# One hybrid RG-LRU and mLSTM layer: the whole body in a scheduled block of the more detailed timing model

## The chip, the core and the metric

The kernel runs on one core of a Trainium2 chip. The metric is the time of one execution on the device in microseconds, the median of the runs shown. The engines are named as the profile names them: PE (TensorE) for matmuls, DVE (VectorE), ACT (ScalarE), POOL (GpSimd), SP (SyncE). Each takes its own instructions in a fixed order and waits on semaphores for the others. In this kernel SP issues the loads and POOL the stores.

## The reference

One layer (DEPTH 1) with a 1024-token prompt and eight single decode tokens, all float32. `D_MODEL` is 1024, there are four mLSTM heads of 256, and the RG-LRU has 1024 channels in 16 gate blocks of 64.

```python
hn = rmsnorm(x, g_norm)
u = hn @ w_in                                   # 1024 x (7*1024 + 8)
xa, za, uq, uk, uv, uo, zb, ui, uf = jnp.split(u, SPLIT_IDX, axis=-1)
yA, hA, bufA = rglru_branch(xa, conv0, h0, ...) # conv of 4 taps, two gates, linear scan over time
hB, C, n, m = mlstm_seq(q, k, v, ig, lf, C0, n0, m0)   # chunks of 128 tokens, state C 256 x 256 per head
yB = jax.nn.sigmoid(uo) * hB
yB = yB * lax.rsqrt(jnp.mean(yB * yB, axis=-1, keepdims=True) + EPS) * g_mhead
merged = jnp.concatenate([yA * silu(za), yB * silu(zb)], axis=-1)
x = x + merged @ w_out
y = rmsnorm(x, g_final)
```

This is done once for the prompt, from zero states, and once for the eight decode tokens, each from its own stored states. For decode token b and head h the new state is C' = scale * C + outer(weighted k, v); it is an output, and q is multiplied by it.

## The kernel before

**Matmuls.** Every float32 operand is split into a rounded high half and a rest: `split` (L70 a copy on ACT, L71 a subtraction on DVE), and `mm3` (L64 high by high, L65 and L66 high by low and low by high) adds three matmuls into one PSUM tile. PSUM has three tiles of tag `o`, two of `kv`, and one each of `tr`, `s` and `qp`; an instruction that writes one of these waits until its last reader is through.

**The input projection** runs over 14 `UNITS` ("v0v1 x0y0 q0k0 x1y1 ..."), two pieces of 256 columns each. A unit is multiplied in a 2 x 2 block scheme with seven products (`Q_P1` to `Q_P7`) instead of eight. `load_raw` (L223, SP) brings its weights in pieces of 512 KB into raw0 and raw1; `prep` makes the seven combined weight blocks (DVE L261, L262, L264, L270) and splits each into `wh` and `wl`, two products ahead of the one that PE runs (`LEAD`, with `NWS` 6 buffers); `evac` (L307 to L332) takes sums out of PSUM and `emit_out` (L343 to L360) stores them from POOL to scratch in DRAM. `dec_unit` multiplies the decode tokens by the same raw weights: sixteen narrow matmuls L236 into the one `tr` tile, a copy L239 on ACT, four transposes L244.

**Background work** is written between the halves of the products, taken from queues of small steps by `pop_bg`. `rg_half` is the RG-LRU of 128 channels and 512 tokens: convolution (L761 to L767), gate matmuls L784 into the `s` and then the `tr` tile, gate outputs L734 on ACT, decay and scan (L797 to L816). `rg_dec` is its decode part (PE L836, four small L734). L659 belongs to the gate preparation of the mLSTM.

**Decode states.** `decode_steps(h)` goes through the eight tokens of a head. `fetch_C` (L909, SP) brings a state of 256 KB into one of four buffers of tile `Cb`, `fetch_v` (L903, SP) broadcasts v into one of two `vbc`. A token is scaled on ACT (L930), gets two additions on DVE (L932) and is stored from POOL (L934). After every second token a run of eight narrow matmuls (L951) multiplies the two states by q into `ps_qp`.

```python
def token(b):
    ...
        A.mul(C, C, dGI[:, b, h:h + 1])                        # L930
        for kb in range(2):
            V.scalar_tensor_tensor(C[:, kb, :], vb_, ...)      # L932
        stq(s_C[0, b, h].rearrange(...), C)                    # L934
        if b % 2:
            late.append(lambda: late.append(products))         # L951
        else:
            fetch_C(i + 2); fetch_C(i + 3)                     # L909
```

**The last stages.** The mLSTM goes over eight chunks and four heads: `m_a` (L1124 to L1134), `m_b` (matmuls L64 to L66 into `ps_qp`, scaled by L1180 into `hh`), normalisation, `m_z` (L1230). In the first of its chunks `wo_prep` still prepares w_out: loads `oraw` of 512 KB (L1246), the decode tokens' product L1260 into `ps_tr`, the split L1269 on ACT and L1270 on DVE. `out_part` multiplies by w_out.

**What sets the order.** The body only states the operations in a program order. The framework underneath schedules them: among the instructions that could run, it takes them by program order against a timing model, and writes one queue for each engine with the semaphore waits that the tiles need. The engine and queue of every instruction are set by the code; no order is written out by hand beyond the program order.

Of the kernel before, what the change touches and what calls it, by code (L numbers as in the profile page):

```python
# [49 lines left out]
def hymba_kernel(  # L50
# [3 lines left out]
    w_rgate, b_rgate, w_igate, b_igate, lru_lambda, b_mi, b_mf, g_mhead, w_out, g_final,  # L54
    y_p, y_s, p_h, p_conv, p_C, p_n, p_m, s_h, s_conv, s_C, s_n, s_m,
):
    nc = tc.nc
    V, A, G, TE = nc.vector, nc.scalar, nc.gpsimd, nc.tensor
    ld = nc.sync.dma_start
    stq = nc.gpsimd.dma_start  # L60
# [1513 lines left out]
```

## Time and profile before

| what | value |
|---|---|
| median of 3 runs | 953.24 us (953.04 to 954.88) |
| span of the profiled execution | 952.8 us |
| DMA | 153.19 MB, mean 161 GB/s |
| matmul L64 into ps_kv, 128x512 | 320, mean 400 ns each |
| split of a weight block, L70 and L71 | 91 each, mean 1049 and 1220 ns |
| scaling of a decode state, L930 | 32, median 723 ns |

A row of the timeline has start and length in us, engine, line, operation and tiles; in brackets stands the idle time of the engine before it and what ended it. Matmuls overlap, so that two follow each other by less than their length. In the rows of waits stand the engine with the tile and line that waited, what it waited for, the total in us, how often, and the longest. The times of a group of instructions are minimum, median and maximum in ns.

### The profile page before, as it was taken

How to read it: one execution, taken by the hardware profiler on the slowest of the kernel's cores; microseconds unless marked ns; L12 is line 12 of the kernel's file. 1: busy time of each engine (PE TensorE's matmuls, PEld its weight loads, DVE VectorE, ACT ScalarE, POOL GpSimd, SP SyncE). 2: the span in 40 equal slices, each digit the busy share in tenths (PEclk: the TensorE clock that was granted, in tenths of full speed). 3: DMA queues.
4: the chain of work that ended last, by engine and by line, in shares of the span. 5: the costliest groups of instructions: out<-in, count | busy, mean ns of one | idle time of the engine just before them, and what ended most of it. 6: DMA issues, size and time to landing. Idle time of an engine off the chain costs nothing.

```text
span 952.8 us, 15351 instructions
## 1 busy us (share of the span) xinstructions
PE 929.8 (98%) x5350; PEld 762.8 (80%) x5350; DVE 711.5 (75%) x1465; ACT 585.0 (61%) x1050; POOL 145.7 (15%) x259
## 2 busy tenths in 40 slices
PE   9999999999999999999999999999989999999997
PEld 7797767777787987777789998866667888888886
DVE  6685798889788877979797867686656676676764
ACT  7563447778677757677687774465446466455532
POOL 1111112111112122111122221010200100000020
PEclk9999999999999999999999999999999999999999
DMA  5521347356645465455647362435963664564361
GB/s 172 183 82 46 132 123 273 110 182 206 238 146 202 156 206 173 164 159 184 213 146 255 119 219 84 153 111 168 302 193 107 185 179 113 154 184 137 120 102 48
DMA packets 131383, 153.19 MB, mean 161 GB/s; under 512 B 15816, under 2 KB 110056, under 8 KB 131298
## 3 DMA queue, kind: packets, MB, share of 16 engines
q1 hardware_dynamic: 113578, 96.34, 34.5%
q0 software_dynamic: 17728, 55.87, 16.3%
q8 instruction: 42, 0.69, 0.3%
q14 instruction: 35, 0.29, 0.1%
HBM read 100.59 MB, written 51.65 MB: 160 GB/s over the span
## 4 chain that ended last, share of the span: by engine, by line
PE 76%; DVE 9%; DMA 7%; issue 4%; ACT 2%; SPq 1%; POOL 0%; DVEq 0%; POOLq 0%; ACTq 0%
PE ps_o L66 12%; PE ps_o L64 12%; PE ps_o L65 12%; PE ps_kv L64 9%; PE ps_kv L66 9%; PE ps_kv L65 9%; PE ps_tr L236 2%; DMA W<-d_alpha 2%; DMA x<-in_x_prompt_dram 2%; PE ps_s L1124 1%; PE ps_qp L951 1%; DVE wl L71 1%; PE ps_tr L1260 1%; PE ps_s L784 1%; PE ps_qp L64 1%
## 5 line engine op out<-in xcount | busy, mean ns | idle before, releaser
L71 DVE TENSOR_TENSOR wl<-raw,wh 128x1024 fp32r<-128x1024 f32 x91 | 111.0, 1220 | 27.6 <-ACT wh L70 19.0
L70 ACT CAST wh<-raw 128x1024 fp32r<-128x1024 f32 x91 | 95.4, 1049 | 58.1 <-PE ps_o L65 23.6
L64 PE MATMUL ps_kv<-cb_hi,wh 128*128 128x512 f32 x320 | 128.1, 400 | 0.6 <-ACT s L317 0.6
L66 PE MATMUL ps_kv<-cb_hi,wl 128*128 128x512 f32 x320 | 125.6, 393 | 0.0
L65 PE MATMUL ps_kv<-cb_lo,wh 128*128 128x512 f32 x320 | 125.2, 391 | 0.0
L64 PE MATMUL ps_o<-cb_hi,wh 128*128 128x512 f32 x240 | 95.0, 396 | 0.0
L66 PE MATMUL ps_o<-cb_hi,wl 128*128 128x512 f32 x240 | 94.1, 392 | 0.0
L65 PE MATMUL ps_o<-cb_lo,wh 128*128 128x512 f32 x240 | 93.5, 389 | 0.0
L64 PEld LDWEIGHTS ps_kv<-cb_hi,wh 128*128 128x128 f32 x320 | 60.1, 188 | 23.7 <-issue 4.6
L66 PEld LDWEIGHTS ps_kv<-cb_hi,wl 128*128 128x128 f32 x320 | 60.1, 188 | 15.6 <-issue 2.5
L65 PEld LDWEIGHTS ps_kv<-cb_lo,wh 128*128 128x128 f32 x320 | 60.2, 188 | 12.5 <-issue 0.8
L64 PE MATMUL ps_kv<-wh,cb_hi 128*128 128x256 f32 x192 | 55.4, 288 | 0.0
L65 PE MATMUL ps_kv<-wl,cb_hi 128*128 128x256 f32 x192 | 54.3, 283 | 0.0
L66 PE MATMUL ps_kv<-wh,cb_lo 128*128 128x256 f32 x192 | 54.3, 283 | 0.0
L64 PE MATMUL ps_o<-wo,rh 128*128 128x512 f32 (+1 forms) x136 | 53.8, 396 | 0.0
L64 PEld LDWEIGHTS ps_o<-cb_hi,wh 128*128 128x128 f32 x240 | 45.1, 188 | 10.6 <-issue 1.7
L66 PEld LDWEIGHTS ps_o<-cb_hi,wl 128*128 128x128 f32 x240 | 45.0, 188 | 10.6 <-issue 0.8
L66 PE MATMUL ps_o<-wo,ml 128*128 128x512 f32 (+1 forms) x136 | 52.1, 383 | 1.1 <-DVE ml L71 1.0
L64 PE MATMUL ps_o<-wo,mh 128*128 128x512 f32 (+1 forms) x136 | 52.8, 389 | 0.0
L65 PEld LDWEIGHTS ps_o<-cb_lo,wh 128*128 128x128 f32 x240 | 45.1, 188 | 9.2
L66 PE MATMUL ps_o<-wo,rl 128*128 128x512 f32 (+1 forms) x136 | 52.0, 382 | 0.0
L65 PE MATMUL ps_o<-wo,rh 128*128 128x512 f32 (+1 forms) x136 | 51.8, 381 | 0.0
(482 smaller groups left out, 2538.7 us busy)
## 6 DMA issues: line engine op xcount, KB each, us to landing
raw<-in_w_in_dram SPq DMA_DIRECT2D x55, 512.0 KB
Cb<-in_state_mlstm_C_dram SPq DMA_DIRECT2D x32, 256.0 KB
out_dram<-Cb POOLq DMA_DIRECT2D x32, 256.0 KB, 4.7
qk<-d_qk SPq DMA_DIRECT2D x32, 256.0 KB
oraw<-in_w_out_dram SPq DMA_DIRECT2D x16, 512.0 KB
d_qk<-s POOLq DMA_DIRECT2D x24, 256.0 KB, 3.9
d_x<-s POOLq DMA_DIRECT2D x16, 256.0 KB, 2.5
zsr<-d_y SPq DMA_DIRECT2D x16, 256.0 KB
```

The lines of the kernel that those rows point to most:

```text
L64: TE.matmul(out, ah, bh, start=first, stop=False, skip_group_check=True)
L65: TE.matmul(out, ah, bl, start=False, stop=False, skip_group_check=True)
L66: TE.matmul(out, al, bh, start=False, stop=last, skip_group_check=True)
L70: A.copy(hi, src)
L71: V.tensor_tensor(lo, src, hi.bitcast(F32), op=ALU.subtract)
L236: TE.matmul(pz[32 * g:32 * g + 32, :], hnd[:, NB * k:NB * k + 32], raws[u, k // 4][:, k % 4, :], start=k < 4, stop=k >= 4, skip_group_chec ...
L784: TE.matmul(pg, w[:, n, :], st["xx"][n], start=k == 0, stop=k == 1)
L951: TE.matmul(pq[32 * g:32 * g + n, 0:256], q, ds_["C", h * NB + bb][:, kb, :], start=b == 1, stop=b == NB - 1, skip_group_check=True)
L1124: TE.matmul(S, qk[:, 2 + kb, :], qk[:, kb, :], start=kb == 0, stop=kb == 1)
L1260: TE.matmul(dec_o[0][32 * g:32 * g + 32, :], md, oraw[m][:, half * 512:(half + 1) * 512], start=n == 0, stop=n == 14, skip_group_check=True)
```

## The change

The kernel's body is put into one block of the framework, entered at its first line, with a flag by which the order of instructions in that block is chosen against another, more detailed timing model of the engines. No operation, tile, size, engine or queue is changed, and the block covers everything from there to the end of the kernel.

```diff
--- before
+++ after
@@ -54,7 +54,7 @@
-    nc = tc.nc
+    nc = (ctx.enter_context(tc.block(schedule_with_timeline_sim=True)), tc.nc)[1]
     V, A, G, TE = nc.vector, nc.scalar, nc.gpsimd, nc.tensor
     ld = nc.sync.dma_start
     stq = nc.gpsimd.dma_start
```

## The prediction

> **What bounds the kernel now.** I read the page first: busy times, then the chain.
>
> ```profile
> span 952.8 us, 15351 instructions
> PE 929.8 (98%) x5350; PEld 762.8 (80%) x5350; DVE 711.5 (75%) x1465; ACT 585.0 (61%) x1050; POOL 145.7 (15%) x259
> ...
> PE 76%; DVE 9%; DMA 7%; issue 4%; ACT 2%; SPq 1%; POOL 0%; DVEq 0%; POOLq 0%; ACTq 0%
> ```
>
> PE sets the end: 929.8 of 952.8 us are busy, and 23 us are all that a better order could remove. How it runs by stage (stretch, its length, busy us of PE, weight loads, DVE, ACT and POOL, granted clock, DMA share, GB/s), and what it waits for:
>
> ```profile
> 100.00:200.00 100.00, 96.26 (x458) 74.30 (x457) 87.34 (x169) 62.40 (x95) 16.30 (x31) 1.00 0.51 168
> 200.00:300.00 100.00, 100.00 (x483) 77.46 (x482) 88.50 (x150) 74.25 (x105) 21.23 (x37) 1.00 0.61 201
> 400.00:500.00 100.00, 100.00 (x543) 80.30 (x542) 84.98 (x140) 71.52 (x102) 17.17 (x30) 1.00 0.52 168
> 600.00:700.00 100.00, 95.88 (x450) 67.70 (x449) 66.88 (x127) 54.81 (x84) 11.02 (x21) 0.98 0.56 182
> ```
>
> ```profile
> PE ps_qp L64 <- ACT hh L1180: 4.0, 1, 4.0
> PE ps_s L784 <- DVE xh L778: 1.7, 2, 1.3
> PE ps_s L659 <- DVE stk L651: 1.7, 1, 1.7
> ```
>
> From 200 to 300 and from 400 to 500 us PE never stops, with DVE at 85 to 88%: there a new order has nothing to win and much to lose. The three named waits come to 4.0 + 1.3 + 1.7 = 7.0 us. The first also costs clock:
>
> ```profile
> 688.00:696.00 8.00, 3.98 (x28) 2.48 (x27) 3.98 (x8) 3.15 (x7) 0.00 (x0) 1.00 0.98 307
> 696.00:700.00 4.00, 4.00 (x20) 3.71 (x19) 3.73 (x9) 1.91 (x6) 0.00 (x0) 0.57 0.58 147
> 140.00:150.00 10.00, 8.68 (x39) 6.82 (x38) 7.68 (x14) 7.32 (x11) 1.45 (x2) 1.00 1.02 300
> ```
>
> After the stall before 696 PE gets a clock of 0.57 for 4 us, so 0.43 x 4 = 1.7 us more are lost; after the shorter stall inside 140:150 it stays at 1.00. The long one costs 4.0 + 1.7 = 5.7 us.
>
> **What the change moves.** Both kernels hold the same instructions; their compiled order, which is known before a run, differs in 1182 of PE's 5035 places, 636 of DVE's 1465, some 316 of ACT's 938, 101 of SP's 385 loads and 59 of POOL's. No instruction gets cheaper. Each engine takes its queue in order, so a price is what an instruction put in front has to wait for. Four moves matter.
>
> **Move 1: the decode of the first heads is bunched.** A head has eight tokens: a 256 KB state is fetched into one of four Cb buffers (L909), scaled on ACT (L930), added to twice on DVE (L932), stored from POOL (L934) and multiplied on PE (L951, a run of eight for two tokens). The buffer is fetched again when store and product are through.
>
> ```profile
> L951 PE MATMUL ps_qp<-Cb,qsel x24: 379/379/380, 216.6 to 253.8; 128*4 128x256 f32 x24
> L932 DVE SCALAR_TENSOR_TENSOR Cb<-vbc,kw,Cb x12: 456/478/486, 210.9 to 244.1; 128x256 f32<-128x256 f32 x12
> L951 PE MATMUL ps_qp<-Cb,qfirst x8: 379/391/403, 197.3 to 197.6; 128*32 128x256 f32 x8
> L930 ACT ACTIVATE Cb<-Cb,dGI x8: 707/724/728, 202.6 to 259.6; 128x512 f32<-128x512 f32 x8
> DMA to landing us min/median/max: 3.1/4.4/4.8
> DMA to landing us min/median/max: 3.1/4.7/7.4
> ```
>
> (The landings: all decode transfers of 195:260, then the stores L934 of 130:270.) Before, head 0's four products are spread from 197.3 to 253.8 us, and its scalings and the next head's first four reach to 259.6. In the new order all four stand within some 80 places of PE, the first ahead of the L784 that PE runs at 164.2 us, the last before 182; eight scalings stand on ACT ahead of a weight copy that had none of them in front of it:
>
> ```profile
> 165.03 1.28 ACT L734 ACT_TABLE_LOAD   x1
> 168.34 0.68 ACT L734 ACTIVATE rg<-ps_tr,hb 64x512 f32<-64x512 f32 x1
> 169.76 0.82 ACT L797 ACTIVATE na<-rg,sp 128x512 f32<-128x512 f32 x1
> 171.78 0.59 ACT L239 COPY Z<-ps_tr 128x512 f32<-128x512 f32 x1 [0.19 <-PE ps_tr L236]
> 174.28 1.05 ACT L70 CAST wh<-raw 128x1024 fp32r<-128x1024 f32 x1 [0.59 <-DVE raw L262]
> 181.10 1.09 ACT L734 ACTIVATE dgr<-ps_s,hb 64x8 f32<-64x8 f32 x4
> ```
>
> ```profile
> 175.42 1.22 DVE L71 TENSOR_TENSOR wl<-raw,wh 128x1024 fp32r<-128x1024 f32 x1
> 164.22 0.39 PE L784 MATMUL ps_s<-xh,ghi 128*128 128x512 f32 x1
> 182.06 0.39 PE L64 MATMUL ps_o<-cb_hi,wh 128*128 128x512 f32 x1
> ```
>
> The row of 164.22 marks where the bunch begins. The copy of 174.28 (with its low half, DVE from 175.42 to 176.6) feeds the PE product of 182.06: PE has 182.1 - 176.6 = 5.5 us to spare. I follow the new order by hand, starting when PE reaches the first product. A step costs its row; a fetch 3.6 us (between the shortest 3.1 and the median 4.4, which also holds stores), a store 0.7 of issue and 4.7. (1) 164.5 product, fetch of the third pair lands 168.3, scaling to 169.0. (2) table load 1.28, the square root 0.6, second scaling 0.72: 171.6. (3) its two DVE additions, 0.96 by the row's duration: 172.6. (4) store, 0.7 + 4.7: 178.0. (5) the fetch that reuses the buffer, for the next head: 181.6. (6) scaling 0.72, four dgr outputs 1.09, a copy 0.3, two L734 of 0.68: 185.1. On these two waits L236's run on PE, since there is one ps_tr buffer; its place is at PE time 182.1 + about 1.1 already lost, so PE is now 3.0 late. (7) scaling 0.72, two activations of 0.82, the run of L236 beside them, L239 0.59, two L307 of 0.59, the eighth scaling 0.72: 190 at the latest step. (8) the copy 1.05: 191. Its reader's place is now 184.3 (182.1 plus the products moved in front): 6.7 late. (9) Its low half comes behind five small DVE steps and ends at 193.3, for a place at 185.2: 8.1 late. (10) The next piece has L264 and the square root with its table ahead of it and ends some 2 us later than its reader: about 10 late in all. PE does not win this back, since 200:300 leaves it no idle time. Bounds: with the shortest fetch throughout and the DVE steps beside the waits, 6; with 4.4 for each of three fetches and the late copies of the next pieces, 13. I take **+10**, nearest to the chain as it stands.
>
> The same happens to head 2 and the first half of head 3, at 375 to 410 us: the products stand up to 362 places earlier. There the copies are further ahead of PE; the same walk leaves 0 to 3 us of stall, and the load for a later unit, behind four vbc loads on SP, another 0 to 2. I take **+1.5**, bounds 0 and +5.
>
> **Move 2: two early stalls go.** L659 stands 28 places later and the first L784 43 later, at one place per 0.23 us (the step from row to row below) 6 and 10 us of other products. That removes 1.7 + 1.3 and some 0.15 of restart at each: **-3.3**; at worst -1.5, if half of the wait appears again at the new place.
>
> ```profile
> 250.54 0.39 PE L66 MATMUL ps_o<-cb_hi,wl 128*128 128x512 f32 x1
> 250.77 0.39 PE L64 MATMUL ps_kv<-cb_hi,wh 128*128 128x512 f32 x1
> ```
>
>
> **Move 3: the stall at 691.**
>
> ```profile
> 695.64 0.39 PE L64 MATMUL ps_qp<-vh,ph 128*128 128x258 f32 x1 [4.02 <-ACT hh L1180]
> 693.25 1.15 ACT L1269 ACTIVATE wo<-oraw,gm 128x1024 fp32r<-128x1024 f32 x1 [4.85 <-DMA oraw<-in_w_out_dram]
> 695.12 0.47 ACT L1180 ACTIVATE hh<-ps_qp,gi_t 128x257 f32<-128x257 f32 x1
> ```
>
> PE waits for hh, which stands on ACT behind an L1269 that waits 4.85 us for its load. In the new order L1180 stands ahead of the L1269s and the PE group 108 places earlier. So this wait goes, at best 5.7 us. But the load is no faster: 688:696 shows the DMA engines 0.98 busy, and the L1260 products that need these loads stand only 32 to 40 places later, 7 to 9 us. I take **-3.5**, between 0 (PE meets the load at L1260) and -5.7.
>
> **Move 4: more split runs of narrow matmuls.** The order cuts L236 into 17 runs instead of 15, L1260 into 15 instead of 13, L951 into 19 instead of 16.
>
> ```profile
> 216.57 0.62 PE L951 MATMUL ps_qp<-Cb,qsel 128*4 128x256 f32 x8
> 301.60 1.92 PE L236 MATMUL ps_tr<-raw,hnd 128*32 128x512 f32 x16
> 303.46 0.39 PE L64 MATMUL ps_kv<-wh,cb_hi 128*128 128x256 f32 x1
> 26.48 1.90 PE L236 MATMUL ps_tr<-raw,hnd 128*32 128x512 f32 x10 [0.53 <-DVE hnd L425]
> 28.32 0.66 PE L417 MATMUL ps_s<-idF,x 128*128 128x128 f32 x4
> 29.34 1.06 PE L236 MATMUL ps_tr<-raw,hnd 128*32 128x512 f32 x6
> 30.33 0.39 PE L64 MATMUL ps_o<-wph,b12h 128*128 128x264 f32 x1
> ```
>
> Sixteen L236 in one run take 303.46 - 301.60 = 1.86 us; cut into 10 and 6 they take 1.84 + 0.99, so one cut costs up to 0.97. I price an L1260 cut alike, and an L951 cut at 0.4, two thirds of its whole run of 0.62. 2 x 0.97 + 2 x 0.97 + 3 x 0.4 = 5.1 at most, and half of that if a cut falls between equal halves; I take **+4**, bounds 2.5 and 5.1.
>
> **The rest.** At the start the transposes of x stand 44 to 48 places earlier, and in the last stage the first products of each output block 31 to 41; both wait for loads or DVE results as before: **0**, bounds -3 and +3. The new order also alternates more often between the accumulations of two PSUM tiles. I cost that at nothing: from ps_o to ps_kv, 250.54 to 250.77, PE keeps its step.
>
> **The sum**, against the profiled 952.8: +10 + 1.5 - 3.3 - 3.5 + 4 + 0 = +8.7, so 961.5; the median of the runs, 953.24, lies 0.4 above the profiled span: **962**. All low ends: 6 + 0 - 3.3 - 5.7 + 2.5 - 3 = -3.5, 949 to 950. All high ends: 13 + 5 - 1.5 + 0 + 5.1 + 3 = +24.6, 978.
>
> The Trainium skill ("TensorE: Matmul & The Clock Gate", Part 1: The HAM clock gate) says that one idle window of about 3.4 us puts the array to half rate, and that it takes about 3.4 us of work to return. The rows above agree: a stall of 4.0 us cost clock, one of 1.3 did not. By that rule the 6.7 us of lateness in move 1 would cost 1.7 us more if they fell in one piece; as I walk them they fall as 3.0, 3.7, 1.4 and 2, so one half-rate stretch at most, and the sum would be 964.
>
> **The rivals.** (a) *Faster, 947.* The decode is covered after all: if fetches land in 3.1 us and the state copies run in ACT's idle 37% of 100:200, then the 5.5 us to spare are just used up, move 1 costs 2 at most, and 691 gives its full 5.7: 952.8 + 2 + 0 - 3.3 - 5.7 + 2.5 = 948.3, and 947 with 1.5 at the start. For it: ACT is only 62% busy there. Against: the waits are in a row on one queue, and four buffers allow no overlap between pairs. It decides if the copy before 182.06 in the new order starts less than 5.5 us late. (b) *Much slower, 978.* Both bunches cost 10 to 13 us, because the fetches also hold SP's queue ahead of weight loads, and the half clock comes once: 952.8 + 13 + 10 - 3.3 - 0 + 4 + 1.7 = 978. For it: both bunches have the same form and DVE is 85% busy at 400:500. Against: there the copies have more lead. (c) *No change.* The stalls only change places: a gain of 7 at the named waits against 7 in the bunch. It needs terms that cancel to 2 us.
>
> **How the numbers follow.** The forecast (cost of the bunch outweighs the stalls removed) 0.58, (b) 0.13, (c) 0.07, (a) 0.22. Slower by over 0.2% (1.9 us, about what can be told from no change) 0.58 + 0.13 - 0.01 = 0.70, the 0.01 being the tail of the forecast that ends under it; faster 0.22 + 0.01 = 0.23, same 0.07. The forecast's own range is 955 to 974; to hold 8 in 10, it reaches into both rivals: 946 to 979.
>
> **What would show it.** PE waits between 165 and 205 us for ACT's L930 or the copy L70 behind it, some 10 us in all; in 200:300 PE at 100% again; no wait for hh L1180 of 4 us and PEclk at 1.00 around 690; no wait at L659 and L784 near 126 and 143; PE busy time up by about 4 us. I am wrong if PE has no wait over 1 us between 165 and 205, if the hh wait is still there, or if the L909 fetches do not come bunched.

## The result and the profile after

The changed kernel takes 998.7 us, the median of four runs (995.17 to 1004.23), against 953.14 us of the kernel before on the same chip: a ratio of 1.0484, interval 1.0461 to 1.0507. It is slower by 4.8%, some 46 us, and lies above the predicted range of 946 to 979. The profiled execution is the slowest of the four (1004.23 us, mean clock 0.978); the other three had 0.982 to 0.987, so the share of the clock below is on the high side. The span and the busy times of its page:

```profile
span 1002.5 us, 15384 instructions
PE 954.0 (95%) x5350; PEld 775.1 (77%) x5350; DVE 714.2 (71%) x1465; ACT 581.6 (58%) x1050; POOL 146.0 (15%) x259
```

DVE and ACT do the same work as before, to within 4 us (711.5 and 585.0). PE is busy 954.0 instead of 929.8 us with the same 5350 instructions, and idle for 48.5 instead of 23.0. So the 50 us of span come half from waiting (25.5) and half from matmuls that took longer (24.2). Most of the second half is the clock: its mean went from 0.994 to 0.978, which is 0.006 x 952.8 = 5.7 us lost before and 0.022 x 1002.5 = 22.1 now. Where it happens, by stretches of 100 us (columns as before: length, busy us of PE, weight loads, DVE, ACT, POOL, granted clock, DMA share, GB/s):

```profile
100.00:200.00 100.00, 90.77 (x414) 65.77 (x413) 73.88 (x135) 52.07 (x84) 18.40 (x33) 0.94 0.52 171
200.00:300.00 100.00, 94.09 (x418) 73.13 (x417) 80.23 (x134) 64.40 (x89) 15.88 (x28) 0.96 0.44 150
300.00:400.00 100.00, 100.00 (x645) 84.23 (x643) 83.62 (x134) 68.61 (x98) 20.81 (x33) 1.00 0.54 176
700.00:800.00 100.00, 94.22 (x470) 70.32 (x467) 60.21 (x142) 49.70 (x110) 10.30 (x19) 0.97 0.61 192
800.00:900.00 100.00, 92.61 (x502) 79.22 (x502) 60.44 (x189) 50.96 (x135) 6.53 (x12) 0.97 0.50 145
```

The last two stretches in the kernel before:

```profile
700.00:800.00 100.00, 99.64 (x550) 82.28 (x549) 65.36 (x199) 54.38 (x145) 7.61 (x14) 1.00 0.51 151
800.00:900.00 100.00, 98.50 (x560) 84.67 (x560) 67.58 (x206) 55.01 (x148) 6.53 (x12) 1.00 0.52 149
```

The losses are local. 300:400 is full; 100:300 and 700:900 lose 28.3 us to waiting (9.23 + 5.91 + 5.78 + 7.39; 5.6 in the kernel before) and 16 to the clock (0.06, 0.04, 0.03 and 0.03 of 100 us; none to two digits before). What PE waits for, in the view of waits:

```profile
PE ps_s L784 <- DVE xh L778: 8.5, 3, 5.9
PE ps_qp L1230 <- ACT hh L1180: 8.0, 3, 4.4
PE ps_tr L236 <- ACT ig L734: 3.6, 1, 3.6
```

**160 to 200 us, the decode bunch.** ACT and PE in the timeline, the rows with a wait, and the windows around them:

```profile
183.75 1.35 ACT L930 ACTIVATE Cb<-Cb,dGI 128x512 f32<-128x512 f32 x2 [5.50 <-DMA Cb<-in_state_mlstm_C_dram]
...
173.80 0.47 PE L784 MATMUL ps_s<-xh,ghi 128*128 128x512 f32 x1 [2.26 <-DVE xh L778]
188.09 3.51 PE L236 MATMUL ps_tr<-raw,hnd 128*32 128x512 f32 x16 [3.62 <-ACT ig L734]
194.86 0.79 PE L64 MATMUL ps_o<-cb_hi,wh 128*128 128x512 f32 x1 [1.88 <-ACT wh L70]
```

```profile
165.00:180.00 15.00, 12.42 (x52) 7.45 (x48) 10.42 (x20) 10.06 (x14) 5.08 (x8) 0.89 0.79 267
180.00:200.00 20.00, 13.35 (x51) 7.43 (x51) 11.90 (x21) 11.45 (x19) 1.08 (x2) 0.78 0.36 123
```

ACT stands idle for 5.50 us at a decode scaling whose state has not landed; the gate output L734 behind it is late, L236 waits for it, and the weight copy behind that is late too. PE is idle for 2.58 + 6.65 = 9.2 us, and the clock is down to a mean of 0.89 and 0.78; the kernel before has 1.00 from 165 to 200 us.

**260 us.** This stall was not predicted. PE, then ACT just before it:

```profile
248.21 0.39 PE L784 MATMUL ps_tr<-xl,glo 128*128 128x512 f32 x1
256.41 0.39 PE L66 MATMUL ps_o<-cb_hi,wl 128*128 128x512 f32 x1
262.71 0.77 PE L784 MATMUL ps_s<-xh,ghi 128*128 128x512 f32 x1 [5.91 <-DVE xh L778]
...
260.97 0.62 ACT L771 CAST xh<-xc 64x512 fp32r<-64x512 f32 x1 [2.08 <-DVE na L811]
262.52 0.58 ACT L314 COPY s<-ps_o 128x512 f32<-128x512 f32 x1
```

```profile
263.00:270.00 7.00, 7.00 (x24) 5.58 (x24) 3.56 (x5) 5.41 (x8) 1.98 (x4) 0.75 0.39 147
```

5.91 us of wait and 0.25 x 7 = 1.8 of clock: 7.7 us. From the last gate product of one half (248.21) to the first of the next PE has work until 256.41 + 0.23, which is 8.4 us; xh, whose way leads from the one through ACT and DVE to the other, came only after 262.71 - 248.21 = 14.5.

**The last stage.** SP, DVE, ACT and PE of the changed kernel around 850 us, and below the same step of the kernel before, around 806 us:

```profile
846.04 0.39 SPq L1082 DMA_DIRECT2D W<-d_alpha  x1
851.61 0.35 DVE L1104 SCALAR_TENSOR_TENSOR W<-W,be_t,maskT 128x128 f32<-128x128 f32 x1 [5.00 <-DMA W<-d_alpha]
852.00 0.31 ACT L1105 ACTIVATE W<-W 128x128 f32<-128x128 f32 x1 [5.32 <-DVE W L1104]
852.21 0.46 ACT L1180 ACTIVATE hh<-ps_qp,gi_t 128x257 f32<-128x257 f32 x1
852.49 0.69 DVE L1233 TENSOR_TENSOR z<-ps_s,z 128x512 f32<-128x512 f32 x1
852.73 0.44 PE L1230 MATMUL ps_qp<-idF,hh 128*128 128x128 f32 x2 [4.39 <-ACT hh L1180]
```

```profile
805.75 0.39 SPq L1082 DMA_DIRECT2D W<-d_alpha  x1
806.70 0.69 DVE L1233 TENSOR_TENSOR z<-ps_s,z 128x512 f32<-128x512 f32 x1 [0.22 <-PE ps_s L1230]
808.71 0.47 ACT L1180 ACTIVATE hh<-ps_qp,gi_t 128x257 f32<-128x257 f32 x1
810.60 0.35 DVE L1104 SCALAR_TENSOR_TENSOR W<-W,be_t,maskT 128x128 f32<-128x128 f32 x1 [3.21 <-DMA W<-d_alpha]
```

In both, W of the next step takes about 5 us from its load to L1104 (5.57 now, 4.85 before). Before, z and hh, which PE needs at once, stood ahead of it on their queues; now they stand behind it, hh by one place on ACT (L1105, L1180), z by two on DVE (L1104, a split L71, L1233).

### The profile page after: what moved, and what is told of

Same layout as the page of the kernel before. It is cut to its first block, busy times and chain, and to the rows that moved or that the text cites. A ratio compares the mean times of both kernels' runs of the same rounds, so it can differ in the third digit from the quotient of the medians.

```text
span 1002.5 us, 15384 instructions
## 1 busy us (share of the span) xinstructions
PE 954.0 (95%) x5350; PEld 775.1 (77%) x5350; DVE 714.2 (71%) x1465; ACT 581.6 (58%) x1050; POOL 146.0 (15%) x259
## 5 line engine op out<-in xcount | busy, mean ns | idle before, releaser
L70 ACT CAST wh<-raw 128x1024 fp32r<-128x1024 f32 x91 | 95.0, 1047 | 68.0 <-PE ps_kv L65 21.9
L64 PE MATMUL ps_kv<-cb_hi,wh 128*128 128x512 f32 x320 | 128.2, 401 | 0.7 <-DVE s L320 0.6
L71 DVE TENSOR_TENSOR wl<-raw,wh 128x1024 fp32r<-128x1024 f32 x91 | 110.9, 1219 | 20.4 <-ACT wh L70 18.9
L64 PE MATMUL ps_o<-cb_hi,wh 128*128 128x512 f32 x240 | 97.5, 406 | 3.9 <-ACT wh L70 3.9
L65 PE MATMUL ps_o<-cb_lo,wh 128*128 128x512 f32 x240 | 95.7, 399 | 0.0
L64 PEld LDWEIGHTS ps_kv<-cb_hi,wh 128*128 128x128 f32 x320 | 60.6, 190 | 22.4 <-issue 3.0
L64 PEld LDWEIGHTS ps_o<-cb_hi,wh 128*128 128x128 f32 x240 | 46.2, 192 | 18.0 <-ACT wh L70 4.6
L64 PE MATMUL ps_kv<-wh,cb_hi 128*128 128x256 f32 x192 | 54.8, 286 | 0.1
L64 PE MATMUL ps_o<-wo,mh 128*128 128x512 f32 (+1 forms) x136 | 53.9, 396 | 0.8 <-ACT mh L70 0.8
L65 PE MATMUL ps_o<-wo,mh 128*128 128x512 f32 (+1 forms) x136 | 52.8, 389 | 0.0
L64 PE MATMUL ps_o<-wo,rh 128*128 128x512 f32 (+1 forms) x136 | 52.2, 384 | 0.4 <-DMA rh<-d_rm 0.4
L1104 DVE SCALAR_TENSOR_TENSOR W<-W,be_t,maskT 128x128 f32<-128x128 f32 x32 | 11.1, 350 | 57.9 <-DMA W<-d_alpha 57.9
```

Of the source, the lines that this page charges most:

```text
L64: TE.matmul(out, ah, bh, start=first, stop=False, skip_group_check=True)
L65: TE.matmul(out, ah, bl, start=False, stop=False, skip_group_check=True)
L70: A.copy(hi, src)
L71: V.tensor_tensor(lo, src, hi.bitcast(F32), op=ALU.subtract)
L1104: V.scalar_tensor_tensor(W, W, be_t[:, c, h:h + 1], maskT, op0=ALU.add, op1=ALU.min)
```

## The experiments

**The block by itself.**

```diff
-    nc = (ctx.enter_context(tc.block(schedule_with_timeline_sim=True)), tc.nc)[1]
+    nc = (ctx.enter_context(tc.block()), tc.nc)[1]
```

> The block around the body without the flag, so the order is chosen against the usual timing model. Theory A (the other model's order is the cause): the same time as before, 953 within 2 us, and the decode products L951 at their old times (first at 197 us). Rival B (being in a block is the cause, whatever the model): close to 999, slower than before by 40 or more.

953.59 us against 953.62, ratio 1.0003 (0.9982 to 1.0025). The block costs nothing that can be measured; what the flag does to the order is all of the 46 us.

**Holding back what looks guilty, and letting the flag choose the rest.** In `w_hold` the next step's W is held behind L1180 of the step before it; in `d_hold` the decode scalings and products are held behind the last weight copy and product ahead of them in program order; `both_hold` does both.

```diff
@@ w_hold
-        A.mul(hh, qc[:, 0:257], gi_t[:, c, h:h + 1])
+        held = A.mul(hh, qc[:, 0:257], gi_t[:, c, h:h + 1])
+        if n + 1 < 4 * NCH:
+            with tc.issue_after(held.ins):
+                m_w(n + 1)                      # L1104 and L1105 of the next step
@@ d_hold
+                with tc.issue_after(lastA[0].ins):
                     A.mul(C, C, dGI[:, b, h:h + 1])
...
+                    with tc.issue_after(final[0].ins):
                         TE.matmul(pq[32 * g:32 * g + n, 0:256], q, ...)
```

> The changed kernel, with only the W exponential L1105 of the next step held behind L1180 on ACT's queue in the last stage. Theory A (L1180 stands behind an L1105 that waits for a 5 us load, and PE waits for L1180): the waits of L64 and L1230 for hh L1180, 11.3 us in the profile, and the half clock after them go, and the time falls by 10 to 19 us, to 980 to 989. Rival C (the load is late anyway and PE meets it one instruction later, at L1133): falls by less than 4 us, to 995 or more, with the wait named at ps_kv or ps_tr instead.

> The changed kernel, with the decode alone held: each scaling L930 stays behind the last weight copy written before it, each product L951 behind the last mm3 written before it. Theory A (the bunched decode costs at 165 to 205 and around 440): the 17.7 us of lateness gained from 160 to 200 and some 5 at 440 go, so 973 to 980. If the 7.7 us at 256, where the head's additions stood on DVE just before, belong to it too, down to 968. Rival D (the early stage is late for another reason in that order, such as the moved gate products L784): stays above 990.

> Both holds on the changed kernel. Theory A: the two losses are in different stages and add up, so the fall is the sum of the two single falls within 4 us, to 953 to 968. Rival: one of them is only hidden behind the other, and the sum is missed by more than 8 us.

999.88 (1.048, 1.0422 to 1.0537), 1002.98 (1.0507, 1.0476 to 1.0539) and 1008.07 us (1.0558, 1.0527 to 1.059). None of them wins anything. In `w_hold` the wait for hh is met one instruction later, in its view of waits (its L1129 is the next step's m_a, its L1241 the z product):

```profile
PE ps_s L1129 <- DVE z L1241: 8.0, 4, 3.3
```

The hold took effect on ACT's queue; DVE's L1104 stayed ahead of z, so as many as 8.0 us came back. `d_hold` moved the first decode products back, from 160 to 205 us, and its trace shows new waits, one of them of 3.6 us at a decode product for DVE's L932. With a scheduler free to answer, such an edit does not isolate its place.

**Pinning queues.** In these kernels an order is written out for chosen queues and the flag orders the rest. `pin_pe` gives PE the queue of the kernel before, `pin_actdve` ACT and DVE theirs, `pin_dma` SP and POOL theirs.

```diff
+    for names, order in PINS:          # one list for each pinned queue
+        ...
+        for a, b in zip(order, order[1:]):
+            tc.add_manual_dep(seen[b], a, how, reason="pin")
```

> The changed kernel with PE's queue alone pinned to the order that it had before (by order-only edges from each PE instruction to the next); the detailed model chooses the other four queues. Theory A2 (the two holds cost as much as they saved, so the loss is not one instruction on ACT: the new order of PE puts a product close behind the one that it depends on through ACT and DVE, and the round trip does not fit): most of the loss goes, 953 to 968. Rival E (ACT's and DVE's order, with scalings and W steps ahead of what PE needs, costs by itself): at least half of the 46 us stays, 976 or more.

> The changed kernel with ACT's and DVE's queues pinned to their order of before; the detailed model chooses PE, SP and POOL. Theory A2: at least half of the loss stays, 976 or more, with PE waiting for DVE and ACT results at products moved forward. Rival E: 953 to 968.

> The changed kernel with the queues of SP and POOL pinned to their order of before; PE, ACT and DVE as the detailed model chooses. Rival F (loads and stores stand in a bad order, so weights, states and W land late): 953 to 970. Theory A2: 985 to 1003, since the round trips between PE, ACT and DVE stay as they are.

1003.19 (1.053, 1.047 to 1.0591), 1031.21 (1.083, 1.0786 to 1.0873) and 1005.56 us (1.0538, 1.0506 to 1.057). Wherever the flag is left free, it makes an order that loses some 50 us or more. Since that order is a new one each time, these runs do not tell what share of the loss any one queue had.

**The new order in one stage alone.** All five queues are pinned from here on. Each kernel has the changed kernel's order in one stretch, cut where all five queues hold the same instructions in both kernels, and the order of before elsewhere: `first_new` 125 to 304 us in the trace of before, `mid_new` 302 to 638, `wo_new` 638 to 724, `late_new` 724 to the end.

> All five queues pinned: the order of the changed kernel only from 125 to 304 us of the trace of before, the order of before elsewhere. Theory G: the loss of that stretch, 22 us net of the 4 that it wins at 126 and 143 us, so 972 to 982. Rival H: the loss of the early stretch is paid back later by slack, 953 to 965.

> All five queues pinned: the order of the changed kernel only from 302 to 638 us. Theory G: the loss of that stretch, 9.5 us, so 959 to 966, most of it around 440. If bunching the decode of heads 2 and 3 by itself cost what I forecast, 1.5: 954 to 957.

> All five queues pinned: the order of the changed kernel only from 638 to 724 us, where the wait for hh L1180 at 691 us stood. By my forecast for this stall (-3.5, at best -5.7): 947 to 950, faster than both kernels. If its gain was only lateness handed on: 953.

> All five queues pinned: the order of before up to 724 us of its trace (w_out prepared, chunks of the mLSTM from the second on to come), the order of the changed kernel from there to the end. Theory G (each stage's order loses by itself, at round trips between PE and the others that the new order leaves too little other work for): the loss of that stretch in the comparison of the profiles, 22 us, so 971 to 979, with PE waiting for hh L1180. Rival H (the last stage only suffers from what came late out of the earlier ones): within 5 of before, 950 to 958.

| kernel | us | against 953.58 | ratio (interval) |
|---|---|---|---|
| first_new | 975.1 | +21.5 | 1.0227 (1.0195 to 1.0258) |
| mid_new | 965.66 | +12.1 | 1.0112 (1.008 to 1.0145) |
| wo_new | 950.01 | -3.6 | 0.9968 (0.9947 to 0.9989) |
| late_new | 974.14 | +20.6 | 1.0219 (1.0188 to 1.025) |

21.5 + 12.1 - 3.6 + 20.6 = 50.6, against the changed kernel's 45.6. So the losses are made where they appear and add up to within 5 us; the start up to 125 us was not taken alone. No run pins all five queues to the order of before, but `wo_new`, pinned throughout, is no slower than the kernel before, so the pins themselves do not make the losses. One stage of the new order is better than the old: `wo_new` is faster than the kernel before by 0.1 to 0.5%, a small gain, but clear of the noise. Its windows at the place where the kernel before lost the stall of 691 us:

```profile
688.00:696.00 8.00, 7.78 (x48) 4.66 (x46) 6.61 (x13) 6.26 (x11) 0.00 (x0) 1.00 0.96 284
696.00:700.00 4.00, 3.99 (x18) 2.14 (x17) 4.00 (x8) 2.05 (x5) 0.55 (x1) 1.00 0.85 238
```

3.98 us busy and a clock of 0.57 have become 7.78 and 1.00, with the DMA engines as full as they were (0.96 and 0.98): PE had other work while the loads came, and waited only 0.2 us at the products L1260 that need them.

**Single places inside the stages.** With all queues pinned, a few instructions change places and the scheduler can't answer. In these kernels line numbers stand 19 higher than in the kernel before (L1123 is L1104, L1199 is L1180, L1249 is L1230, L1252 is L1233, L89 is L70, L333 is L314).

```diff
@@ late_wswap: late_new, at four places each
-ACT: L1105 L1180
+ACT: L1180 L1105
-DVE: L1104 L71 L1233              (at two of the places with one more between)
+DVE: L71 L1233 L1104
@@ late_wback2: the same, and at those places W goes further back
-ACT: L1180 L1105 L70(v) L70(m)
+ACT: L1180 L70(v) L70(m) L1105
-DVE: L1233 L1104 L1185 L1185 L1187 L71(v) L71(m)
+DVE: L1233 L1185 L1185 L1187 L71(v) L71(m) L1104
```

> As late_new (the new order only from about 724 us to the end), with eight local moves inside the last stage: at the four places where ScalarE's L1105 (the next step's W) stands directly ahead of L1180 the two change places, and at the four places where VectorE's L1104 stands ahead of the z product L1233 it goes behind it. Theory W: the last stage's loss is made where the next step's W, fresh from its load, stands ahead of work that TensorE needs now. late_new's four waits before L1230 (1.5, 4.8, 2.9 and 1.8 us in its trace, less 0.2 us each for the product itself) are 10 us and the half clock behind the two long ones about 1.7 us each: 974.1 - 13.4 = 961 us (958 to 965). The 3.7 us wait at 745 us, which is another place, stays. Rival K: as in w_hold, the wait is met again by the next instruction: 971 to 977 us. Rival S: the loss is a matter of the new order as a whole and not of these places: 974 us.

> As late_wswap, with W moved back one step further at the same four places: ScalarE's L1105 goes behind the two casts L70 (of v and of mh) as well, and VectorE's L1104 behind the state updates L1185, the sum L1187 and the two splits L71 (of v and of ml). In late_wswap's trace the waits before L1230 are gone, and TensorE waits 6.9 us in 4 waits for mh, the next thing behind L1105, with the clock at 0.83 and 0.95 in the two stretches behind them. Theory W, as it stands now: every instruction that TensorE needs soon and that stands behind the late W pays for it, so all of them have to go ahead: 969.6 - 6.9 - 2 = 961 us (958 to 964). Rival K: the wait is handed on once more (to kh, ph or the next hh): 967 to 972 us.

`late_wswap` takes 969.56 us, 1.0172 (1.0144 to 1.02): between the two theories. Its waits and the rows of one place show why:

```profile
PE ps_o L83 <- ACT mh L89: 6.9, 4, 3.2
```

```profile
819.14 0.31 ACT L1124 ACTIVATE W<-W 128x128 f32<-128x128 f32 x1 [4.20 <-DVE W L1123]
819.65 0.61 ACT L89 CAST mh<-z 128x512 fp32r<-128x512 f32 x1
820.32 0.80 PE L83 MATMUL ps_o<-wo,mh 128*128 128x512 f32 x1 [3.21 <-ACT mh L89]
```

The waits of 9.4 us before L1230 are gone, and 6.9 us of them stand at mh, the next thing behind W on ACT. `late_wback2` moves W behind that too: 959.42 us, 1.0053 (1.0034 to 1.0071), the waits for mh are down to one of 0.8 us, and the window in which that step falls runs full:

```profile
820.00:830.00 10.00, 10.00 (x56) 8.64 (x55) 6.63 (x20) 4.92 (x16) 0.00 (x0) 1.00 0.58 159
```

Of the last stage's 0.0219, 0.0166 or 15.8 us came from four W steps that stood a few places too early on two queues; nothing was changed on PE, SP or POOL. A wait of 3.3 us for hh at 745 us, another place, was left.

```diff
@@ first_gate: first_new, TensorE's queue at 260 us
-PE: L784 L784 (28 products L64 to L66)
+PE: (28 products L64 to L66) L784 L784
@@ first_dec: first_new, 160 to 190 us
-ACT: L930 L806 L930 L930 L771 L930 ... L930 L930 L734 x4 L70 L734 L734
+ACT: L806 L930 L930 L771 L930 L930 ... L734 x4 L70 L734 L734 L930 L930
-DVE: L932 L932 L810
+DVE: L810 L932 L932
@@ wo_gate: wo_new, TensorE's queue at 126 and 142 us
-PE: (8 transposes L659) (9 products) ... L784 L784 (1 product) L784 L784 (7 products)
+PE: (9 products) (8 transposes L659) ... (8 products) L784 L784 L784 L784
```

> As first_new (the new order only between about 125 and 304 us), with one move on TensorE's queue: the two gate products L784 that wait 6.1 us for xh at 260 us go behind the 28 products that follow them. Theory P: the loss at 260 us is one of distance, the gate product stands too few products behind the one before it for its way through ScalarE and VectorE; with 28 products of 0.227 us (6.4 us) more between, the wait goes, and the stretch of half clock behind it (13 us at about 0.75): 975.1 - 6 - 3 = 966 us (964 to 969). Rival K: the chain of gates behind it comes later by as much, and the next product waits in its place: 973 to 977 us.

> As first_new, with moves on ScalarE and VectorE between 160 and 190 us alone: ScalarE's square root L806 goes ahead of the two decode steps L930 that wait for their state load, L771 ahead of the last two of that bunch, and two later L930 behind the four gate activations L734; VectorE's L810 goes ahead of two L932. The loads and TensorE's queue are left as they are. Theory B: the bunch costs what the gate chain waits behind decode steps whose loads are late. In first_new's trace TensorE waits 2.7, 3.7, 1.5, 2.3 and 1.1 us between 170 and 195 us; some 2.5 of the first, and 1.7 to 3 of the second go, with a part of the half clock behind them: 975.1 - 5 = 970 us (967 to 972). Rival K: the loads only move, and the decode products on TensorE wait in the gates' place: 974 to 978 us.

> As wo_new (the new order only between 638 and 724 us, else the order of before), with two moves on TensorE's queue: the eight transposes L659 that wait 2.1 us at 126 us go behind the nine products that follow, and the four gate products L784 at 142 us behind the eight that follow. Theory P: both waits are of distance, so 2.07 + 1.57 us less 0.2 us each, and some half clock, go: 950.0 - 3.5 = 946.5 us (945.5 to 948). Rival K: later work waits in their place: 950 us.

`first_gate` wins nothing: 978.89 us, 1.0258 (1.023 to 1.0286), where `first_new` has 1.0227. Its wait at that place:

```profile
PE ps_o L83 <- ACT s L333: 6.4, 1, 6.4
```

The product that came forward needs a PSUM tile that ACT's copy L314 has to empty, and that copy stands behind the cast of xh, as the rows of 260.97 and 262.52 above show. So the theory of distance on PE fell: ACT's queue holds up both. To move the copy ahead of the cast and of the square root L806 before it was not tried. In the changed kernel PE stands idle from 256.8 us, so what that copy reads was ready then, 5.7 us before it ran at 262.52: that move is the untested candidate, and what it would take to mend 260 us is left open.

`first_dec` takes 972.91 us, 1.0199 (1.0171 to 1.0227), 2 to 3 us less than `first_new`, half of what was expected; the two intervals overlap, so a gain is not shown. Two waits of 160 to 200 us, `first_new` first (L255 is L236, L263 is L244):

```profile
PE ps_tr L255 <- ACT ig L753: 3.3, 1, 3.3
PE ps_tr L263 <- ACT Z L258: 0.7, 1, 0.7
```

```profile
PE ps_tr L263 <- ACT Z L258: 2.2, 1, 2.2
PE ps_tr L255 <- ACT ig L753: 1.9, 1, 1.9
```

The wait for the gate's output shrinks by 1.4 us, and 1.5 come back at L244, one step further on. That the decode steps ahead of the gates cost time is read from the changed kernel's trace; this run does not show it.

`wo_gate` takes 949.65 us, 0.9962 (0.9944 to 0.9979), no other than `wo_new`: the two waits of 1.7 and 1.2 us came back as 1.8 and 1.2 at later products (the transpose L882 of the decode tokens' v, and L64). Rival K held.

**All of the new order, with the two mended places.**

> The new order from end to end (the changed kernel's own queues), with the moves of late_wback2 in the last stage and those of first_dec between 160 and 190 us, and nothing else. If the losses of the stages are made at these places and add up, it is the changed kernel less what the two take away by themselves: 998.7 - 13 (974.1 to 961, as expected of late_wback2) - 2 (975.1 to 972.9, first_dec) = 984 us (981 to 988). If the places only stand for an order that is late as a whole: 993 to 1000 us.

983.33 us, 1.0304 (1.0271 to 1.0338): by the ratios 17 us less than the changed kernel, from 13 instructions moved on ACT and DVE. The places make about the same loss in the whole kernel as alone (15.8 us for W; 2.7 for the decode, which alone is not clear of noise). For the other 29 us the runs show the stages; the waits in them are read from the traces, and no mend was found.

## Why the prediction was wrong

**The direction and the first mechanism were right, the size was not.** The forecast was slower, by 8.7 us; it is 46. By stages the sum missed 20.6 us in the last (0 forecast), 14.8 in the first (21.5 against 6.7) and 10.6 in the middle (12.1 against 1.5). By its own terms:

- **The rest, "0, bounds -3 and +3".** This is the step that failed most. It looked at how far the first products of each output block had moved on PE (31 to 41 places) and saw that they "wait for loads or DVE results as before". It did not look at DVE and ACT in the last stage, where L1104 and L1105 had gone ahead of L1233 and L1180 by one or two places. `late_new` puts the last stage at +20.6 us, and `late_wback2` gives 15.8 of them to the four W steps. The view of all engines' waits in the kernel before already showed DVE waiting at this place, before and after in turn:

```profile
DVE W L1104 <- DMA W<-d_alpha: 43.5, 21, 3.7
```

```profile
DVE W L1104 <- DMA W<-d_alpha: 57.9, 28, 5.1
```

- **Move 1, "+10", bounds 6 and 13.** The walk was right as far as it went: ACT waited 5.50 us for a state that had to be fetched into a used buffer, and PE at L236 for the L734 behind it (3.6 us), then for the weight copy (1.9). Of PE's 9.2 us of idle time between 165 and 200 us 2.3 more fell at a gate product L784, which the walk did not have, so that 9.2 lies as near to 10 as it does partly by luck. The sum left out the clock, which cost up to 0.11 x 15 + 0.22 x 20 = 6 us more, where the sentence beside it allowed 1.7. And the walk stopped at 205 us: 260 us, where a gate product came too soon, took 7.7 us that no term held. `first_new` measures the stretch at +21.5, with move 2's gain inside it; the terms gave +10 - 3.3 = 6.7.
- **The second bunch, "+1.5", bounds 0 and +5.** `mid_new` has +12.1 for 302 to 638 us. It is not taken apart, so what failed there stays open; the only wait of PE over 1 us in that stretch of its trace is 2.08 us for a weight copy, the one that the changed kernel has at 446 us, below.
- **Move 2, "-3.3".** The stalls went: 120:130 and 140:150 are full in the changed kernel. What that saved was not measured by itself, and `wo_gate` shows that moving the waiting products alone would not have done it.
- **Move 3, "-3.5", bounds 0 and -5.7.** `wo_new` measures -3.6 (-5.1 to -1.0) for the whole stage. The direction and the place are right; the size partly by luck, since the wait did not come back at L1260 (0.2 us), as the -3.5 had half supposed.
- **Move 4, "+4".** Not measured by itself.

The windows to move 2, in the changed kernel:

```profile
120.00:130.00 10.00, 10.00 (x55) 7.15 (x48) 9.94 (x15) 4.80 (x8) 1.10 (x2) 1.00 0.15 55
140.00:150.00 10.00, 10.00 (x46) 8.26 (x46) 7.64 (x12) 6.27 (x10) 1.62 (x3) 1.00 0.92 291
```

**The signs it named.** The waits between 165 and 205 us came, the 4 us wait at 691 and those at 126 and 143 went. PE at 100% in 200:300 did not come (94.09), nor a busy time up by only 4 us (24.2). Of the rivals, (b) with 978 us was the nearest. Its dear second bunch has some support in `mid_new`'s +12.1, but it had nothing for the last stage, which cost almost as much as the first, and the half clock once, where it came many times. (a) and (c) fell.

## What to carry to other kernels

When a scheduler changes the order, list on every queue, the helpers' too, which instructions with a fresh load or a far product behind them now stand ahead of something the bounding engine needs soon: four steps that stood a few places too early cost 15.8 us here, about 4 us each with the clock behind them. The one wait that was mended here went only when everything that PE soon needed went ahead of the late instruction on both queues; moving less, or moving the waiting product, handed the wait on to the next. And test a new order stage by stage: the best stage of this one is faster than the kernel that it slowed down by 4.8%.

## What was not expected of the hardware

Short waits can already cost clock. Two waits of PE in the changed kernel, 2.06 and 2.36 us, and the stretch behind each:

```profile
446.56 0.50 PE L64 MATMUL ps_o<-cb_hi,wh 128*128 128x512 f32 x1 [2.06 <-ACT wh L70]
889.84 0.33 PE L1230 MATMUL ps_qp<-idF,hh 128*128 128x128 f32 x1 [2.36 <-ACT hh L1180]
```

```profile
447.00:450.00 3.00, 2.91 (x8) 1.74 (x7) 3.00 (x5) 2.98 (x5) 0.00 (x0) 0.56 0.00 0
890.00:894.00 4.00, 3.83 (x16) 3.10 (x16) 4.00 (x12) 1.98 (x6) 0.00 (x0) 0.63 0.65 170
```

Behind 2.06 and 2.36 us the clock is 0.56 and 0.63 for 3 to 4 us; behind a wait of 1.23 us at 926.17 it is 1.00. But the length alone does not decide. The wait of 446.56, for the same weight copy, is as long in `mid_new` and costs no clock there:

```profile
423.63 0.50 PE L83 MATMUL ps_o<-cb_hi,wh 128*128 128x512 f32 x1 [2.08 <-ACT wh L89]
424.00:428.00 4.00, 3.55 (x15) 2.46 (x14) 3.96 (x7) 3.60 (x5) 0.00 (x0) 1.00 0.00 0
```

Nor does one of 1.97 us at 768.90 in the changed kernel (1.00 from 769 to 773), while in the kernel before one of 1.46 us at 38.70 was followed by 0.55 from 41.0 to 44.5, which the prediction did not use. In the traces of these runs every wait of PE of 2.5 us or more is followed by a lower clock; between 1.5 and 2.5 us both happen, and what decides there is not shown. With waits of 2.26, 3.62 and 1.88 us in move 1 the mean clock was 0.89 and 0.78 over 165 to 200 us, where the prediction had one such stretch at most.

The Trainium skill ("TensorE: Matmul & The Clock Gate", Part 1: The HAM clock gate) puts the drop at an idle window of about 3.4 us; the rows above do not agree, they have it also behind waits of 1.5 to 2.4 us, and the measurement decides.
